# One address remainder for the first stage's matmul operands, twelve work tiles, and 8 KB for descriptors

## The chip, the core and the metric

The kernel runs as one program on one core of a Trainium2 chip. The core's engines run side by side and meet only at semaphores: TensorE (PE, with its weight loads shown apart as PEld), VectorE (DVE), ScalarE (ACT), GpSimd (POOL) and SyncE (SP). SP and POOL also issue the DMA transfers between the device memory and the on-chip memory, which has 128 partitions; a tile stands at one byte address in all of them. The metric is the device time of one execution in microseconds (us), from runs that are repeated and compared with each other.

## The reference

Two layers act on x of 2048 tokens by 1024 features, in float32, with a last RMSNorm behind them. Cut to what matters here:

```
u = rmsnorm(x, ln_g[0])
proj = u @ w_in                      # 1024 -> 3*2048 + 8: xm, z, o_pre, i_pre, f_pre
xc = silu(causal_dwconv(xm, conv_w, conv_b))
q, k = per head xc @ w_q, xc @ w_k;  v = per head xm @ w_v
h = mlstm_chunkwise(q, k, v, log_i, log_f)         # matrix memory, head by head
y = (layernorm(sigmoid(o_pre) * h) * norm_w + skip * xc) * silu(z)
x = x + y @ w_out
# second layer: rmsnorm, w_in (1024 -> 2*1536), conv, block gates, linear scan, w_out
out = rmsnorm(x, final_g)
```

The change lies in the first line of matrix work, `proj = u @ w_in`.

## The kernel before, in words

**Stages.** `phase_a1` computes the first layer's norm and `proj`, and is what this document calls the first stage; its results xm, xc = silu(conv(xm)), silu(z) and sigmoid(o) go to device memory. `phase_a2` does heads, memory and output of the first layer; the second layer and the final norm follow. The second layer uses the same class `Slab` for its big products, with `paired=True`.

**Products.** A float32 product is made of three matmuls on halves that TensorE reads as float32r: `split_into` (L806, L809) gives hi = round(t) on ACT and lo = t - hi on DVE, and `mm3` (L391 to L393) adds hi*hi, hi*lo and lo*hi into one PSUM bank. The 2x2 blocks of a matrix product go through a scheme with seven block products instead of eight. Its seven combinations of the activations, `u11 t2 t3 u21 t1 t4 u22`, are split once per half of the tokens into standing places of 2048 bytes, h and l for each of four 128-row pieces. The weights and their sums are split into a ring of eight slots (tile `s`), hi and lo one behind the other; the four sums are stored by POOL for the second half of the tokens (`keep`, L123) and fetched back by SP then (`kept`, L128).

**Wide and narrow.** `group` and `early` make xm and z: weights from a slot stand still and a 512-column place moves past them ("wide", `pa pb pc pd <- u11h..., s`). Each of the seven products is four pieces of three matmuls, 32 times: 384 matmuls, 2688 in all. `o_group` makes o and the gates: here pieces of the places stand still and 258 columns of a slot move ("narrow", `oa ob oc od <- s, u11h...`), 2688 again; its slots hold 516 columns, so `slot(516)`.

**Work tiles.** The ring `wk` of ten tiles of 516 columns holds partial sums (`p1`, `u2`, `u3`), xm with its three history columns, xc, z and the stores of o. xm, xc and z leave through POOL's queue, and a tile comes free when its store has landed.

**Order.** The tile framework's scheduler sets the order on each engine from the order in the code, from `tc.high_priority()` and from the added edges of `order`. PE, ACT, DVE, POOL and SP then each run their list in order.

**Places.** Pools are laid out upwards from address 0 behind a block of 16,384 bytes for the descriptors that POOL writes for its DMAs; the pool `tu` (the `u11` places) lies at the upper end. A tile is rounded up to a multiple of 32 bytes, so a slot of 2*516 floats takes 4128 and a tile of 516 floats 2080.

Of the kernel before, what the change touches and what calls it, by code (L numbers as in the profile page):

```python
# [7 lines left out]
F32 = mybir.dt.float32  # L8
F32R = mybir.dt.float32r
# [5 lines left out]
P = 128  # L15
# [3 lines left out]
TB = 512  # L19
# [29 lines left out]
class Slab:  # L49
# [38 lines left out]
        return (self.ta if nm in ("t3", "u22", "t1", "t4") else self.tp).tile([P, 2 * TB], dtype, tag=f"{nm}{j}", name=f"{nm}{j}")  # L88

    def wk(self, name):  # L90
        return self.rg.tile([P, 516], F32, tag="wk", name=name, bufs=10)

    def wkr(self, name):
        return self.rg.tile([P, 516], F32R, tag="wk", name=name, bufs=10)

    def psum(self, name):
        return self.pm.tile([P, 512], F32, tag="mm", name=name)

    def slot(self, w=512):

        return self.sl.tile([P, 2 * self.wide], F32R, tag="s", name="s")[:, 0:2 * w]

    def raw(self):
        return self.rw.tile([P, self.wide], F32, tag="raw", name="raw", bufs=8)[:, 0:512]
# [58 lines left out]
        return out  # L163

    def invrms(self, acc):
        rc = self.rg.tile([P, 4], F32, tag="rc", name="rc", bufs=4)
        self.K.stats_sum(self.rg, self.pm, acc if isinstance(acc, list) else [acc], rc, "mm")
        return rc

# [7 lines left out]
    def place(self, nm, j):  # L177
        if self.paired:
            self.other.pop((nm, j), None)
            t = self.pair(nm, j, F32R)  # L180
            return t[:, 0:TB], t[:, TB:2 * TB]
        n = 516 if nm == "t3" else TB
        home = self.tu if nm == "u11" else self.tp
        return tuple(home.tile([P, n], F32R, tag=f"{nm}{x}{j}", name=f"{nm}{x}{j}") for x in "hl")


    def take(self, nm, j):
# [21 lines left out]
    def temp(self, nm, x, j):  # L209

        if self.paired:
            if (nm, j) not in self.other:
                t = self.pair(nm, j)
                self.other[nm, j] = {"h": t[:, 0:TB], "l": t[:, TB:2 * TB]}
            return self.other[nm, j].pop(x)
        self.places.pop((nm, j), None)
        return self.tp.tile([P, 516 if nm == "t3" else TB], F32, tag=f"{nm}{x}{j}", name="temp")[:, 0:TB]

    def x(self):
        return self.rx.tile([P, TB], F32, tag="x", name="x", bufs=8)  # L220
# [117 lines left out]
class Trunk:  # L338
# [75 lines left out]
    def phase_a1(self, xT, woq, wxz, wout, D):  # L414
        tc, nc = self.tc, self.nc
        with ExitStack() as ctx:
            S = Slab(self, ctx, "g0")
            tp, rg, pm = S.tp, S.rg, S.pm
            wk, psum = S.wk, S.psum
            S.fix()  # L420
            G = tp.tile([P, 2, 64], F32, name="G")
            hist = tp.tile([P, 16, 3], F32, name="hist")
            nc.vector.memset(hist, 0.0)
            NE = 6
            first = [2 * m + 1 for m in range(NE)]
# [98 lines left out]
            def squares(xs, t1=False):  # L524
                acc = S.temp("t1", "l", 0) if t1 else wk("acc")[:, 0:TB]
                for k, x in enumerate(xs):
                    if k == 0:
                        nc.scalar.activation(acc, x, AF.Square)
                    else:
                        sq = S.temp("t1", "l", 1 + k % 3) if t1 else wk("sq")[:, 0:TB]  # L530
                        nc.scalar.activation(sq, x, AF.Square)
                        self.summed = nc.vector.tensor_tensor(acc, acc, sq, op=ALU.add)
                return acc
# [131 lines left out]
            for k in range(KD):  # L665
                S.scale(xs, None, pb, (k,))
                nm = ("u11", "u21")[k // 4]
# [3 lines left out]
            for s in range(2):  # L671
# [12 lines left out]
                for j, (kind, i) in enumerate(middle):  # L684
# [21 lines left out]
                    if s or j < len(middle) - 1:  # L706
                        n2 = {}
                        if s == 0 and j == len(middle) - 3:
                            rc = []
# [1242 lines left out]
```

## Time and profile before

| | |
|---|---|
| three runs | 2852.49, 2856.59, 2860.08 us (median 2856.59) |
| the profiled execution | 2854.54 us; its span from first to last instruction 2852.8 us |
| granted TensorE clock | 0.996 of full speed |
| PE busy | 2802.1 us, 98% of the span |
| DVE, ACT, POOL busy | 2131.6, 1515.6, 453.3 us (75%, 53%, 16%) |
| DMA | 687.38 MB, mean 241 GB/s |

The page gives the busy time of each engine, the span in slices, the DMA queues and the chain of waits that ended last. A matmul's duration in the profile is longer than its distance to the next one, since matmuls overlap; the distance from start to start is what a long row of them costs. A row of groups gives a mean, a row of one tile's instructions the shortest, the median and the longest.

### The profile page before, as it was taken

To read this page: it belongs to the slowest core of one execution; us is meant where nothing else is said; L and a number is where in the kernel's file an instruction comes from. 1 tells how busy PE (TensorE), PEld (TensorE's weight loads), DVE (VectorE), ACT (ScalarE), POOL (GpSimd) and SP (SyncE) were. 2 spreads that over 40 slices of the span, in tenths; PEclk is the share of its full clock that TensorE was granted. 3 is DMA by queue.
4 is the path that set the end of the run, shared out by engine and by line. 5 is a ranking of instruction groups with operands and counts; after the bars stand their busy time and mean duration, and the time that the engine had idled before them with its cause. 6 is when DMAs were issued, how large, how long until landed. Compare 5 with 4: busy or idle time off the path is not lost.

```text
span 2852.8 us, 43314 instructions
## 1 busy us (share of the span) xinstructions
PE 2802.1 (98%) x15442; PEld 2427.4 (85%) x15442; DVE 2131.6 (75%) x3657; ACT 1515.6 (53%) x2577; POOL 453.3 (16%) x846
## 2 busy tenths in 40 slices
PE   7999999999999999999999999999999999999998
PEld 5799987889997889999999988888788888788886
DVE  7767779735658688888888876678889657777774
ACT  6444545523444466666666643435444323977771
POOL 1211123111212211111121121101221111000000
PEclk9999999999999999999999999999999999999999
DMA  6756677667988765656576578776776765888866
GB/s 234 273 212 230 237 255 259 210 210 265 317 306 286 252 202 196 196 187 212 170 237 202 178 273 295 278 240 219 256 253 231 235 203 179 316 312 308 286 222 206
DMA packets 292472, 687.38 MB, mean 241 GB/s; under 512 B 29088, under 2 KB 103584, under 8 KB 292256
## 3 DMA queue, kind: packets, MB, share of 16 engines
q1 hardware_dynamic: 225072, 451.13, 49.4%
q0 software_dynamic: 66608, 232.43, 21.4%
q8 instruction: 122, 2.00, 0.3%
q10 hardware_dynamic: 576, 1.05, 0.1%
q14 instruction: 94, 0.77, 0.1%
HBM read 447.32 MB, written 237.17 MB: 240 GB/s over the span
## 4 chain that ended last, share of the span: by engine, by line
PE 80%; issue 8%; DVE 5%; ACT 2%; DMA 2%; POOL 2%; POOLq 0%; DVEq 0%; SPq 0%; ACTq 0%
PE pc L391 4%; PE pc L392 4%; PE pc L393 4%; PE pd L391 4%; PE pd L392 4%; PE pd L393 4%; PE pa L391 4%; PE pj L392 4%; PE pj L391 4%; PE pa L393 4%; PE pj L393 4%; PE pa L392 4%; PE acc L392 2%; PE acc L393 2%; PE acc L391 2%
## 5 line engine op out<-in xcount | busy, mean ns | idle before, releaser
L806 ACT CAST s<-raw 128x512 fp32r<-128x512 f32 (+1 forms) x280 | 172.7, 621 | 262.7 <-PE pd L393 74.0
L809 DVE TENSOR_TENSOR s<-raw,s 128x512 fp32r<-128x512 f32 (+1 forms) x280 | 191.7, 687 | 55.0 <-ACT s L806 54.0
L391 PE MATMUL acc<-yh,wr 128*128 128x512 f32 x384 | 148.4, 391 | 2.3 <-ACT R L1673 1.1
L392 PE MATMUL acc<-yl,wr 128*128 128x512 f32 x384 | 149.9, 390 | 0.2 <-DVE yl L809 0.2
L806 ACT CAST u<-t 128x512 fp32r<-128x512 f32 x112 | 69.1, 620 | 151.5 <-PE pc L393 47.3
L393 PE MATMUL acc<-yh,wr 128*128 128x512 f32 x384 | 149.5, 389 | 0.0
L732 DVE SCALAR_TENSOR_TENSOR xc<-xm,vec,xc 128x512 f32<-128x512 f32 x192 | 139.2, 746 | 5.6 <-ACT xc L731 4.1
L809 DVE TENSOR_TENSOR u<-t,u 128x512 fp32r<-128x512 f32 x112 | 77.1, 689 | 76.4 <-ACT u L806 76.4
L806 ACT CAST s<-sum 128x512 fp32r<-128x512 f32 (+1 forms) x120 | 74.1, 618 | 110.1 <-PE pc L393 41.3
L391 PE MATMUL pa<-u,s 128*128 128x512 f32 x304 | 119.0, 392 | 0.8 <-ACT y L1163 0.8
L393 PE MATMUL pa<-u,s 128*128 128x512 f32 x304 | 118.5, 390 | 0.1
L392 PE MATMUL pa<-u,s 128*128 128x512 f32 x304 | 118.6, 390 | 0.0
L1092 DVE SCALAR_TENSOR_TENSOR C<-C,dl,kv 128x516 f32<-128x516 f32 x112 | 83.7, 748 | 45.0 <-PE kv L393 45.0
L732 DVE SCALAR_TENSOR_TENSOR xc<-xr,vec,xc 128x512 f32<-128x512 f32 x144 | 105.8, 746 | 8.9 <-ACT xc L731 7.5
L391 PE MATMUL pj<-vwh,xmh 128*128 128x512 f32 x256 | 102.3, 402 | 0.0
L806 ACT CAST Ch<-C 128x516 fp32r<-128x516 f32 x120 | 72.5, 622 | 54.7 <-DVE da L1114 41.8
L392 PE MATMUL pj<-vwl,xmh 128*128 128x512 f32 x256 | 100.2, 391 | 0.1
L393 PE MATMUL pj<-vwh,xml 128*128 128x512 f32 x256 | 100.0, 391 | 0.0
L809 DVE TENSOR_TENSOR s<-sum,s 128x512 fp32r<-128x512 f32 (+1 forms) x120 | 82.3, 687 | 21.4 <-ACT s L806 20.5
L391 PEld LDWEIGHTS acc<-yh,wr 128*128 128x128 f32 x384 | 71.9, 188 | 19.1 <-ACT R L1673 1.6
L391 PE MATMUL pd<-u,s 128*128 128x512 f32 x224 | 87.3, 390 | 0.0
L392 PE MATMUL pd<-u,s 128*128 128x512 f32 x224 | 87.2, 389 | 0.0
(501 smaller groups left out, 10013.3 us busy)
## 6 DMA issues: line engine op xcount, KB each, us to landing
wr<-d_ow SPq DMA_DIRECT2D x96, 512.0 KB, 4.3
d_wx<-s POOLq DMA_DIRECT2D x64, 512.0 KB, 4.4
s<-d_wx SPq DMA_DIRECT2D x64, 512.0 KB, 4.7
s<-d_ws SPq DMA_DIRECT2D x64, 512.0 KB, 6.6
raw<-in_wxz_dram SPq DMA_DIRECT2D x124, 256.0 KB, 4.8
d_wr<-s POOLq DMA_DIRECT2D x48, 512.0 KB, 3.8
s<-d_wr SPq DMA_DIRECT2D x48, 512.0 KB, 4.5
raw<-in_rwin_dram SPq DMA_DIRECT2D x94, 256.0 KB, 4.2
```

The source lines that it names most:

```text
L391: mm(out, sh, mh, start=first, stop=False, skip_group_check=resumed)
L392: mm(out, sh, ml, start=False, stop=False, skip_group_check=resumed)
L393: mm(out, sl, mh, start=False, stop=last, skip_group_check=resumed)
L732: self.convd = [nc.vector.scalar_tensor_tensor(out, x[:, j:j + TB], self.v(wn, m * 4 + j), out, op0=ALU.mult, op1=ALU.add) for j in range( ...
L806: a = nc.scalar.copy(hi, src)
L809: b = (nc.gpsimd if lo_eng == "p" else nc.vector).tensor_tensor(lo, src, hi.bitcast(F32), op=ALU.subtract)
L1092: v = nc.vector.scalar_tensor_tensor(C2, C2, self.dl[:, r:r + 1], p2, op0=ALU.mult, op1=ALU.add)
```

## The change

Everything applies to the first stage alone (`paired` false), but for the last line.

1. A slot becomes 1088 floats (4352 bytes) instead of 1032 (4128). A narrow slot's contents begin 8 floats (32 bytes) into it.
2. The `t3` places are 512 floats like the others, instead of 516.
3. A work tile becomes 528 floats (2112 bytes) instead of 516 (2080 with rounding), and the ring has twelve instead of ten.
4. `hist` (the convolution's history) and `rc` (four floats of the norm, now six tiles) move into the pool `tu`, below which the `u11` places then begin 384 bytes lower.
5. The descriptor block takes 8192 bytes instead of 16,384, which pays for the larger rings.

The order of instructions on every engine is the same, row for row. What the built program's addresses come to, modulo 256:

| tile | before | after |
|---|---|---|
| t2, u21, t1, t4, u22 places | 96 | 96 |
| t3 places (eight) | 96 128 160 192 224 0 32 64 | 96 |
| u11 places | 224 | 96 |
| weight slots (eight) | 96 128 160 192 224 0 32 64 | 96 |
| narrow slots' contents | as the slots | 128 |
| raw weights, weight sums | all multiples of 32 | all multiples of 32 |
| second layer's places and slots | 96 | 96 |

```
     def wk(self, name):
-        return self.rg.tile([P, 516], F32, tag="wk", name=name, bufs=10)
+        return self.rg.tile([P, 516 if self.paired else 528], F32, tag="wk", name=name, bufs=12 - 2 * self.paired)[:, 0:516]
 
     def wkr(self, name):
-        return self.rg.tile([P, 516], F32R, tag="wk", name=name, bufs=10)
+        return self.rg.tile([P, 516 if self.paired else 528], F32R, tag="wk", name=name, bufs=12 - 2 * self.paired)[:, 0:516]
...
     def slot(self, w=512):
 
-        return self.sl.tile([P, 2 * self.wide], F32R, tag="s", name="s")[:, 0:2 * w]
+        o = 0 if w <= 512 else 8
+        return self.sl.tile([P, 1024 if self.paired else 1088], F32R, tag="s", name="s")[:, o:o + 2 * w]
...
     def invrms(self, acc):
-        rc = self.rg.tile([P, 4], F32, tag="rc", name="rc", bufs=4)
+        rc = (self.rg if self.paired else self.tu).tile([P, 4], F32, tag="rc", name="rc", bufs=4 if self.paired else 6)
...
             return t[:, 0:TB], t[:, TB:2 * TB]
-        n = 516 if nm == "t3" else TB
         home = self.tu if nm == "u11" else self.tp
-        return tuple(home.tile([P, n], F32R, tag=f"{nm}{x}{j}", name=f"{nm}{x}{j}") for x in "hl")
+        return tuple(home.tile([P, TB], F32R, tag=f"{nm}{x}{j}", name=f"{nm}{x}{j}") for x in "hl")
...
-        return self.tp.tile([P, 516 if nm == "t3" else TB], F32, tag=f"{nm}{x}{j}", name="temp")[:, 0:TB]
+        return self.tp.tile([P, TB], F32, tag=f"{nm}{x}{j}", name="temp")
...
-            hist = tp.tile([P, 16, 3], F32, name="hist")
+            hist = S.tu.tile([P, 16, 3], F32, name="hist")
...
-    nc = _bacc.Bacc("TRN2", target_bir_lowering=False, num_devices=1)
+    nc = _bacc.Bacc("TRN2", target_bir_lowering=False, num_devices=1, dynamic_dma_scratch_size=8192)
```

## The prediction

> **What bounds the kernel now.** I read the page's head first, then engine time by stage, then PE's groups in the first stage and in the second layer, then PE's waits.
>
> ```profile
> span 2852.8 us, 43314 instructions
> PE 2802.1 (98%) x15442; PEld 2427.4 (85%) x15442; DVE 2131.6 (75%) x3657; ACT 1515.6 (53%) x2577; POOL 453.3 (16%) x846
> ...
> PE 80%; issue 8%; DVE 5%; ACT 2%; DMA 2%; POOL 2%; POOLq 0%; DVEq 0%; SPq 0%; ACTq 0%
> ```
>
> ```profile
> core 0: us, PE busy (x) PEld busy (x) DVE busy (x) ACT busy (x) POOL busy (x), PEclk, DMA share, GB/s
> ...
> 20.00:993.00 973.00, 962.73 (x5435) 834.25 (x5435) 670.91 (x1319) 448.88 (x792) 192.88 (x355) 1.00 0.74 253
> 993.00:1650.00 657.00, 650.54 (x4705) 613.65 (x4705) 570.16 (x1024) 444.15 (x845) 113.77 (x244) 0.99 0.60 197
> 1650.00:2853.00 1203.00, 1184.86 (x5289) 975.86 (x5287) 881.73 (x1295) 612.40 (x926) 144.60 (x241) 1.00 0.75 255
> ```
>
> The first stage runs from about 20 to 993 us. In these 973 us PE stands still for about 10; DVE is busy for 69%, ACT for 46%, and the DMA engines for 74% of the time. PE sets this stage's length, and what one of its matmuls costs is worth its full count. A work tile or a descriptor matters only where PE waits for it.
>
> **Wide matmuls: the first stage against the second layer.** The same form, 128 rows by 512 columns with weights from a slot, at the same granted clock (1.00 in both rows above). First the groups of the first stage, then those of the second layer; the three numbers are the shortest, median and longest duration in ns:
>
> ```profile
> L391 PE MATMUL pb<-t2h,s x128: 388/394/796, 58.4 to 978.1; 128*128 128x512 f32 x128
> L392 PE MATMUL pc<-t3l,s x128: 387/394/797, 59.4 to 981.1; 128*128 128x512 f32 x128
> ...
> L393 PE MATMUL pd<-u22h,s x128: 388/394/400, 93.8 to 992.5; 128*128 128x512 f32 x128
> ```
>
> ```profile
> L391 PE MATMUL pa<-u,s x304: 387/389/504, 1658.5 to 2429.6; 128*128 128x512 f32 x152
> ...
> L393 PE MATMUL pd<-u,s x224: 389/389/390, 1747.7 to 2442.3; 128*128 128x512 f32 x112
> ```
>
> In the second layer nearly every one takes 389 ns, and 390 is the longest of 224. In the first stage the median is 394, though single ones reach 387. The program is the same there, class and all; what differs is where the tiles stand. In the second layer all places and slots begin at 96 modulo 256; in the first stage the slots run through all eight multiples of 32, and t3 and u11 stand off 96. One slot in eight happens to match. Two whole products of the first stage, the timeline's starts in us, the first with its weights in the slot at 64, the second in the slot at 96, the operand at 96 both times:
>
> ```profile
> 112.13 0.39 PE L391 MATMUL pd<-u22h,s 128*128 128x512 f32 x1
> ...
> 114.93 0.39 PE L391 MATMUL pd<-t1h,s 128*128 128x512 f32 x1
> ```
>
> ```profile
> 928.76 0.39 PE L391 MATMUL pc<-t4h,s 128*128 128x512 f32 x1
> ...
> 931.48 0.39 PE L391 MATMUL pd<-u22h,s 128*128 128x512 f32 x1
> ```
>
> Twelve matmuls in 2.80 us are 233 ns from start to start, twelve in 2.72 us are 227. Is that traffic of the other engines? A view of engine time over these two products, with a third between whose slot is at 64 too:
>
> ```profile
> 112.10:114.90 2.80, 2.80 (x13) 2.25 (x12) 1.34 (x2) 1.26 (x2) 0.98 (x2) 1.00 0.90 336
> 202.50:205.20 2.70, 2.70 (x13) 2.20 (x12) 2.63 (x10) 1.92 (x3) 0.55 (x1) 1.00 0.00 2
> 928.70:931.45 2.75, 2.75 (x14) 2.28 (x13) 2.67 (x6) 0.66 (x2) 0.71 (x2) 1.00 0.86 337
> ```
>
> The quick product has DVE busy throughout and DMA at 337 GB/s; the slow ones have DMA once at 336 and once at 2 GB/s. Neither engines nor transfers sort them; the remainder of the weights' address does. A match does not act at once: a product at 426.6 us with operand and slot both at 96 shows
>
> ```profile
> L391 PE MATMUL pc<-t4h,s 128*128 128x512 f32 x4 | 1.6, 394 | 0.0
> L392 PE MATMUL pc<-t4l,s 128*128 128x512 f32 x4 | 1.6, 393 | 0.0
> L393 PE MATMUL pc<-t4h,s 128*128 128x512 f32 x4 | 1.6, 392 | 0.0
> ```
>
> a mean of 393, between 395 and 389. Matched products seem to settle over some six to eight matmuls to an even pace and to lose it at the next mismatched slot. That is why one matching slot in eight gains little now, and why the whole ring at one remainder may gain more than eight times as much.
>
> **The change, part by part.**
>
> *Places and slots at one remainder (wide).* After the change every wide operand and every slot stands at 96 modulo 256, as in the second layer. Seven products of 384 matmuls are 2688; 394 - 389 = 5 ns each gives 13.4 us. Bounds: nothing, if placement isn't the cause; 2688 x 6 ns (233 against 227) = 16 us if most are like the product at 112 us. After waits and narrow products the pace has to settle again; the second layer has such breaks too (504 is one) and keeps its median. I take 13 us.
>
> [...]
>
> *Narrow products.* The stationary places are at 96 before and after, u11 apart; the moving contents go from mixed remainders to 128. The group rows of the first stage, the slot that happens to stand at 128 now (a stretch near 759 us), and the narrow form of the next stage:
>
> ```profile
> L391 PE MATMUL od<-s,u22h 128*128 128x258 f32 x128 | 36.2, 283 | 0.0
> L392 PE MATMUL od<-s,u22h 128*128 128x258 f32 x128 | 36.1, 282 | 0.0
> ...
> L392 PE MATMUL oa<-s,u21h 128*128 128x258 f32 x3 | 0.8, 281 | 0.0
> L393 PE MATMUL oa<-s,u21l 128*128 128x258 f32 x2 | 0.6, 282 | 0.0
> ...
> L392 PE MATMUL kv<-vl,kh 128*128 128x258 f32 x236 | 67.4, 286 | 0.4 <-DVE vl L1058 0.4
> ```
>
> The nearest row is the slot at 128: about 1 ns less on 2688 matmuls, a gain of 2.7 us. The ends: 2 ns less (281 against 283), a gain of 5.4 us; and kv, with other remainders on both sides, 3.5 ns more, a loss of 9.4 us. I take a gain of 3, by the nearest row.
>
> *Twelve work tiles.* Waits in the first stage for a tile whose store is on its way:
>
> ```profile
> PE oa L391 <- ACT p L591: 1.9, 3, 0.7
> ...
> ACT p L591 <- DMA d_xm<-xm: 11.3, 3, 5.1
> ```
>
> ACT has to copy the first narrow partial sum into a work tile whose xm is still being stored; it is late by up to 5.1 us, and behind it PE waits for PSUM three times. With two more tiles the store has about two tiles' time longer. Of 1.9 us and the weight loads and the pace lost around it I take 2; the bounds are 0 and 3. What the copy then waits for is PE's own product, as at its other calls.
>
> *Descriptor block.* Half the room for what POOL writes per DMA:
>
> ```profile
> L641 POOL DMA_DIRECT2D d_sz<-z x64 | 35.0, 547 | 181.4 <-ACT z L639 181.4
> ...
> q0 software_dynamic: 66608, 232.43, 21.4%
> d_xm<-xm POOLq DMA_DIRECT2D x64, 256.0 KB, 4.9
> ```
>
> POOL spends 0.55 us on an issue and lands it 4.9 us later; in the first stage it is busy for 193 of 973 us and waits for ACT's results, not for room. I cost it at nothing. That cover is POOL's idle time: were each issue to wait for the landing before it, the stage's 355 POOL rows (x355 above), nearly all DMAs, would need 355 x 5.4 = 1900 us, twice the stage; with two in flight 960, about the stage; with four 480, hidden again.
>
> *The rest.* `hist` and `rc` are the same instructions on another address: nothing. No instruction moves on any engine. In the next stages all pools keep their remainder; the tiles that take over first-stage addresses at 993 us are freed by other tiles than before. PE loses about 6 us in that whole stage, and I see no term there.
>
> **Sum.** 13 + 3 + 2 = 18 us off the profiled execution's own 2854.5 us is 2836.5. The median of the three runs, 2856.6, stands 2 us above that execution; against it I forecast 2838 us.
>
> **The rivals.**
>
> *A. As above*: 2838, own range 2832 to 2844. For it: the exact pace in one matching product and in the whole second layer. Chance 0.82.
>
> *B. Placement does nothing for PE here.* The even pace would come from something else that the second layer has. Then the work tiles' 2 us are all: 2854 to 2855. Against it: the three windows above. Chance 0.06. [...]
>
> *C. The narrow products lose what the wide ones gain in part.* At 128 they go to the pace of kv: 13 + 2 - 9.4 = about 6 us, 2851. For it: kv's own remainders cost it 3 to 4 ns. Against: the slot at 128. Chance 0.05.
>
> *D. Another engine takes up half of it.* PE comes 1.8% sooner to each product, and splits by ACT and DVE or transfers become the last to arrive: about 9 us, 2847. Against: 10 us of PE waits in 973, DVE at 69%; DMA at 74% would go to 75%. Chance 0.04.
>
> *E. Slower: the descriptor room holds back POOL's queue.* With fewer than two DMAs in flight, work tiles come free later, ACT's p copies and with them PE wait at each of the eight `o_group` calls for a landing, 4.9 us: 39 us on 2838, about 2877. It decides from the point at which issue to landing over the number in flight exceeds 973 / 355 = 2.7 us. For it: the room is halved. Against: POOL's idle time is put down to ACT throughout. Chance 0.03.
>
> **How the numbers follow.** A measurement of this kernel tells about 0.3%, 8.6 us, from no change. Faster by more than that: A, most of D: 0.85. Within it: B, C and the rest of D: 0.12. Slower: E, 0.03. The range 2829 to 2849 takes in the narrow products at their best (16 + 5.4 + 3 = 24.4 us off, and 3 to 4 us by which the three runs stray from their median) below and D above; outside it lie B, C and E with 0.14, and little of A.
>
> **What would show it.** Wide groups of the first stage at a median of 389 with a shortest of 388 or 389, and the stage's end near 975 us instead of 993: right. Medians of 391 to 393: the pace settles only in part. Narrow groups at 281 or 282 means: right; 285 and above is C. No row of PE or ACT p waiting on d_xm: the twelve tiles. POOL issues still at 0.54 us, with no row in which POOL waits on its own DMAs: the descriptor block at nothing. A stage that shortens by 18 us with later stages that lengthen would make the forecast wrong in a place that I cost at nothing.

## The result, and the profile after

The changed kernel takes 2841.22 us (median of six runs, 2838.34 to 2844.68); the kernel before, run beside it, 2855.07 us (six runs, 2851.08 to 2860.08). The ratio is 0.9952, with a 95% interval of 0.9943 to 0.9962: faster by 13.9 us, where 18 were forecast and 2838 us predicted. The profiled execution is the shortest of the six, 2838.34 us; the profiled one before took 2854.54. Between these two, from which the accounts below are made, lie 16.2 us.

The head of the page of the changed kernel: span, busy time of each engine, and the chain of waits.

```profile
span 2836.6 us, 43324 instructions
PE 2785.1 (98%) x15442; PEld 2421.6 (85%) x15442; DVE 2129.8 (75%) x3657; ACT 1515.7 (53%) x2577; POOL 451.8 (16%) x846
...
PE 81%; DVE 7%; issue 5%; DMA 3%; ACT 2%; POOL 1%; POOLq 0%; DVEq 0%; SPq 0%; ACTq 0%
```

PE is busy for 17 us less with the same 15442 matmuls; DVE, ACT and POOL do what they did. The view of engine time by stage, with the first stage cut at 975 us, where the prediction wanted its end:

```profile
core 0: us, PE busy (x) PEld busy (x) DVE busy (x) ACT busy (x) POOL busy (x), PEclk, DMA share, GB/s
20.00:975.00 955.00, 944.55 (x5420) 828.41 (x5419) 665.59 (x1313) 446.82 (x789) 191.82 (x353) 1.00 0.75 256
975.00:1632.00 657.00, 649.82 (x4716) 612.68 (x4715) 572.57 (x1028) 444.97 (x846) 112.42 (x244) 1.00 0.61 198
1632.00:2836.00 1204.00, 1186.10 (x5294) 976.42 (x5292) 882.24 (x1296) 613.06 (x926) 145.52 (x243) 1.00 0.74 255
```

The granted clock is 1.00 in this stage as before. 5420 matmuls fit into these 955 us, where the kernel before had 5435 in 973. The first matmul of the second stage starts at 978.4 us; before, at 992.8. So 14.4 of the 16.2 us come from the first stage. The wide groups, shortest, median and longest duration in ns:

```profile
L391 PE MATMUL pb<-t2h,s x128: 389/389/796, 58.3 to 964.1; 128*128 128x512 f32 x128
L392 PE MATMUL pc<-t3l,s x128: 389/389/793, 59.3 to 967.0; 128*128 128x512 f32 x128
...
L393 PE MATMUL pd<-u22h,s x128: 388/389/397, 94.2 to 978.2; 128*128 128x512 f32 x128
```

These are the second layer's 389, in place of 394. The narrow ones in the view that gives busy time and mean duration:

```profile
L391 PE MATMUL od<-s,u22h 128*128 128x258 f32 x128 | 36.0, 282 | 0.0
...
L392 PE MATMUL od<-s,u22h 128*128 128x258 f32 x128 | 36.0, 281 | 0.0
...
L393 PE MATMUL od<-s,u22l 128*128 128x258 f32 x128 | 35.8, 280 | 0.0
```

**Start to start.** Durations overlap: a wide matmul of the changed kernel lasts 389 ns in the median, and the next one starts 227 ns after it. What PE pays is the distance from one matmul's start to the next. I worked it out for the 2688 wide and the 2688 narrow matmuls of each trace. A distance of 300 ns or more after a wide one, of 150 or more after a narrow one, is called a pause (what it has over the pace counts); the mean of the others is the pace.

| | before | after | difference in the stage |
|---|---|---|---|
| wide pace | 232.34 ns | 227.33 ns | -13.5 us |
| narrow pace | 119.94 ns | 118.89 ns | -2.8 us |
| pauses between narrow matmuls | 3.6 us (7) | 1.1 us (4) | -2.5 us |
| pauses between wide matmuls | 16.1 us (49) | 21.3 us (69) | +5.2 us |
| first product starts at | 19.9 us | 19.3 us | -0.7 us |

Before rounding the sum is -14.4, as is the shift of the stage's end. The first three rows are the prediction's three terms, 13, 3 and 2. The fourth it did not have. The waits of PE's weight loads in the first stage (total us, times, longest) say who is late, first before, then after:

```profile
PEld oa L391 <- ACT p L591: 2.5, 3, 0.9
...
PEld pa L391 <- ACT p L312: 0.7, 3, 0.3
...
PEld pd L391 <- DVE xm L302: 0.5, 2, 0.3
```

```profile
PEld pa L391 <- ACT p L312: 1.6, 5, 0.5
...
PEld pd L391 <- DVE xm L302: 1.2, 3, 0.6
```

The wait for the work tile (`p` of L591) is gone. The waits for a copy or an add that empties a PSUM bank have grown, each short: the two rows shown by 1.6 us together. The rest of the 5.2 us is spread over many short pauses. One of the grown waits in the timeline of the changed kernel (start and length in us, engine):

```profile
205.02 1.53 DVE L732 SCALAR_TENSOR_TENSOR xc<-xm,vec,xc 128x512 f32<-128x512 f32 x2
...
206.46 0.68 DVE L302 TENSOR_TENSOR xm<-pd,p 128x512 f32<-128x512 f32 x1
...
207.20 0.19 PEld L391 LDWEIGHTS pd<-u22h,s 128*128 128x128 f32 x1 [0.56 <-DVE xm L302]
```

PE wants to write bank `pd` again, but DVE first does two steps of the convolution (1.53 us) and only then the add that empties the bank (0.68 us); PE's weight load waits 0.56 us for it. In the kernel before, the same add ended at 207.16 us and the weight load started at 207.84, without a wait: here the PE that comes sooner waits longer. That the other pauses grew for the same reason is not shown one by one.

In the rest of the program the two executions differ by 2.6 us in the second stage and by 0.8 us, the other way, behind it. That is not the change: among the kernels below, which leave the second stage alone, its length differs by more than that.

### The profile page after: what moved, and what is told of

Its sections match the earlier page's. It is cut to its first block, busy times and chain, and to the rows that moved or that the text cites. A ratio compares the mean times of both kernels' runs of the same rounds, so it can differ in the third digit from the quotient of the medians.

```text
span 2836.6 us, 43324 instructions
## 1 busy us (share of the span) xinstructions
PE 2785.1 (98%) x15442; PEld 2421.6 (85%) x15442; DVE 2129.8 (75%) x3657; ACT 1515.7 (53%) x2577; POOL 451.8 (16%) x846
## 4 chain that ended last, share of the span: by engine, by line
PE 81%; DVE 7%; issue 5%; DMA 3%; ACT 2%; POOL 1%; POOLq 0%; DVEq 0%; SPq 0%; ACTq 0%
PE pc L391 4%; PE pd L391 4%; PE pc L392 4%; PE pc L393 4%; PE pd L393 4%; PE pd L392 4%; PE pj L392 4%; PE pj L391 4%; PE pj L393 4%; PE pa L391 4%; PE pa L393 4%; PE pa L392 4%; PE acc L392 2%; PE acc L393 2%; PE acc L391 2%
## 5 line engine op out<-in xcount | busy, mean ns | idle before, releaser
L391 PE MATMUL pa<-u,s 128*128 128x512 f32 x304 | 119.0, 392 | 0.8 <-ACT y L1163 0.8
L809 DVE TENSOR_TENSOR s<-sum,s 128x512 fp32r<-128x512 f32 (+1 forms) x120 | 82.3, 687 | 20.3 <-ACT s L806 19.9
L391 PEld LDWEIGHTS acc<-yh,wr 128*128 128x128 f32 x384 | 71.9, 188 | 19.8 <-DMA wr<-d_ow 1.9
```

What stands on the lines that cost most here:

```text
L391: mm(out, sh, mh, start=first, stop=False, skip_group_check=resumed)
L809: b = (nc.gpsimd if lo_eng == "p" else nc.vector).tensor_tensor(lo, src, hi.bitcast(F32), op=ALU.subtract)
```

## The experiments

Each kernel ran in three or five rounds beside the kernel before, whose median was between 2855.9 and 2856.4 us. Each edit is against the changed kernel unless it says otherwise. The differences named for narrow blocks are bytes by which a block's address stands beyond that of the stationary place, modulo 256.

| kernel | wide: slot against place | narrow blocks | tiles | wide pace, ns | narrow pace, ns | pauses, wide / narrow, us | stage ends, us | median, us | ratio to before (95%) |
|---|---|---|---|---|---|---|---|---|---|
| before | mixed | mixed | 10 | 232.34 | 119.94 | 16.1 / 3.6 | 992.8 | 2855.07 | |
| after | same | 32 to 56 | 12 | 227.33 | 118.89 | 21.3 / 1.1 | 978.4 | 2841.22 | 0.9952 (0.9943 to 0.9962) |
| slots at 64 | 224 | 32 to 56 | 12 | 233.28 | 119.03 | 17.5 / 1.1 | 991.2 | 2853.83 | 0.9995 (0.9986 to 1.0004) |
| slots alternate | same, 128 | mixed | 12 | 230.42 | 120.15 | 19.8 / 1.0 | 988.3 | 2850.36 | 0.9982 (0.9973 to 0.9991) |
| all at 0 | same | 32 to 56 | 12 | 227.22 | 118.90 | 21.7 / 1.1 | 978.6 | 2837.56 | 0.9941 (0.9926 to 0.9956) |
| all at 0, again | same | 32 to 56 | 12 | 227.25 | 118.90 | 22.4 / 1.1 | 979.4 | 2839.42 | 0.994 (0.9926 to 0.9953) |
| ten tiles | same | 32 to 56 | 10 | 227.22 | 118.90 | 21.4 / 4.5 | 981.6 | 2843.51 | 0.9958 (0.9944 to 0.9972) |
| before, twelve tiles | mixed | mixed | 12 | 232.32 | 120.02 | 17.5 / 1.0 | 991.4 | 2853.03 | 0.999 (0.9981 to 0.9999) |
| before, 8 KB | mixed | mixed | 10 | 232.28 | 119.94 | 17.8 / 2.8 | 992.7 | 2856.45 | 0.9997 (0.9988 to 1.0006) |
| narrow at 0 | same | 0 to 24 | 12 | 227.24 | 122.70 | 21.3 / 1.0 | 988.7 | 2852.00 | 0.9989 (0.998 to 0.9997) |
| narrow at 64 | same | 64 to 88 | 12 | 227.22 | 120.04 | 23.0 / 1.0 | 984.1 | 2846.11 | 0.9962 (0.9949 to 0.9976) |
| narrow at 224 | same | 224 to 248 | 12 | 227.40 | 119.05 | 21.2 / 1.1 | 979.1 | 2841.53 | 0.9948 (0.9936 to 0.9961) |
| narrow, two pieces | same | 32, 40 | 12 | 227.16 | 120.00 | 26.8 / 1.0 | 986.7 | 2848.59 | 0.9972 (0.9963 to 0.9982) |
| narrow, four pieces | same | 32 | 10 | 227.25 | 120.00 | 27.9 / 21.8 | 1009.1 | 2871.39 | 1.0055 (1.0041 to 1.0069) |

### What the wide products need: slots at 64, slots that alternate, everything at 0

*Slots at 64.* All wide contents begin 224 bytes into the slot, so that every slot stands at 64 and every place at 96. Everything else is the change.

```
-        o = 0 if w <= 512 else 8
+        o = (0 if self.paired else 56) if w <= 512 else 8
```

> The changed kernel, but the wide contents begin 224 bytes into their slot, so all wide weights stand at 64 modulo 256 against operand places at 96; nothing else moves. Theory P (what counts is that weights and moving operand share one remainder modulo 256): the wide medians go from 389 back to 394 or 395, the stage by 2640 x 5 to 6.6 ns = 13 to 17 us, 2854 to 2858 us in all. Rival C (it is enough that all slots share one remainder with each other, whichever): medians stay at 389 and the time at 2841. Rival N (the gain came from the ring sizes or the descriptor block): 2841 as well.

*Slots that alternate.* Slots of 4224 bytes, which stand at 96 and 224 in turn; the places stay at 96.

```
-        return self.sl.tile([P, 1024 if self.paired else 1088], F32R, tag="s", name="s")[:, o:o + 2 * w]
+        return self.sl.tile([P, 1024 if self.paired else 1056], F32R, tag="s", name="s")[:, o:o + 2 * w]
```

> The changed kernel, but a slot takes 4224 bytes, so the eight slots stand at 96 and 224 modulo 256 in turn, all at 96 modulo 128; places at 96. Theory P with a period of 256: about half of the wide products match and settle only late in their twelve matmuls, the others run at 232 to 233 ns from start to start; a mean near 231, some 10 to 12 us lost, 2851 to 2854 us. Rival with a period of 128: medians 389, 2841 us.

*Everything at 0.* Two pads move all places and slots of the first stage, and of the second layer, to remainder 0.

```
+        self.pad = cp.tile([P, 40], F32, name="pad")
+        nc.vector.memset(self.pad, 0.0)
...
+            nc.vector.memset(S.tu.tile([P, 24], F32, name="padu"), 0.0)
```

> The changed kernel, but 160 bytes of padding ahead of the low pools and 96 in the upper pool, so places and slots of the first stage, and those of the second layer, stand at 0 modulo 256, equal to each other. Theory P (only the equality counts): medians 389 in both, 2841 us within 3. Rival A (the remainder 96 itself counts): medians near 394 in the first stage and in the second layer, (2688 + 5088) x 5 ns = 39 us more, 2880 us.

One wide group of each, in this order (shortest, median, longest duration in ns; first and last start):

```profile
L391 PE MATMUL pd<-u22h,s x128: 393/396/505, 94.3 to 990.5; 128*128 128x512 f32 x128
```

```profile
L391 PE MATMUL pd<-u22h,s x128: 387/392/504, 93.9 to 987.6; 128*128 128x512 f32 x128
```

```profile
L393 PE MATMUL pd<-u22h,s x128: 387/389/499, 94.0 to 978.0; 128*128 128x512 f32 x128
```

Slots that all stand at one remainder, but not at that of the places, give no quick pace: 396 ns in the median, slower even than the mixed ring's 394. So it isn't that the addresses stay the same from slot to slot. With alternating slots half the matmuls have a match: those 1356 are 228.2 ns apart, the other 1269, at a distance of 128 bytes, 232.8. So the period is not 128; and half a ring of matches gives about half of what lies between the slots at 64 (233.3) and the change (227.3). Nor is the period longer than 256: the changed kernel's slots are 17 x 256 bytes apart, so that neighbours differ by 256 modulo 512, and the pace over all of them is 227.3 ns. Everything at 0 keeps the pace of 227.2, and the second layer, which was moved with it, its 389, so it is not remainder 96 itself. What is left is the prediction's cause: weights and moving operand with one remainder modulo 256 gave the quick pace, 227.2 to 227.3 ns here. The slots at 64 have the change's twelve tiles, narrow placing and descriptor room as well, and with them no more than a ratio of 0.9995: the tiles and the narrow products earn little more than the wide pace loses against the mixed ring. All three medians lie just under what the theory of equal remainders expected, by 0.2 to 0.6 us.

An equal remainder is not the only good one, though. The ring of the kernel before runs through all eight differences; by the addresses of the built program its wide matmuls have these paces:

| slot minus place, modulo 256 | 0 | 32 | 64 | 96 | 128 | 160 | 192 | 224 |
|---|---|---|---|---|---|---|---|---|
| pace in the kernel before, ns | 229.7 | 232.7 | 233.0 | 233.5 | 232.7 | 233.2 | 230.1 | 233.5 |

The two other kernels with a mixed ring agree: with twelve tiles 229.5 at 0 and 230.8 at 192, with 8 KB alone 229.6 and 230.0. So a slot 64 bytes below its operand is nearly as quick there as one at the same remainder. No run has a whole ring at 192; what pace it would settle to is open.

### The work tiles and the descriptor room

*Ten tiles.* The change with ten work tiles of 528 floats; a pad keeps the remainders.

```
-        return self.rg.tile([P, 516 if self.paired else 528], F32, tag="wk", name=name, bufs=12 - 2 * self.paired)[:, 0:516]
+        return self.rg.tile([P, 516 if self.paired else 528], F32, tag="wk", name=name, bufs=10)[:, 0:516]
...
+            nc.vector.memset(rg.tile([P, 32], F32, tag="pad", name="padr", bufs=1), 0.0)
```

> The changed kernel with ten work tiles instead of twelve and a pad that keeps every remainder. If the two tiles are worth what the first trace's waits say, PE's waits for the copy of the first narrow partial sum come back, 2 to 3 us: 2843 to 2845 us, with the wide medians at 389. If they are worth nothing: 2841. If the gain was theirs and not the places': 2853.

The waits come back, of PE and, behind it, of ACT (from 600 us to the stage's end):

```profile
PE oa L391 <- ACT p L592: 2.1, 4, 0.7
```

```profile
ACT p L592 <- DMA d_xm<-xm: 9.3, 2, 4.7
```

Narrow pauses are 4.5 us against 1.1, the stage ends 3.2 us later, the median is 2.3 us higher.

*The kernel before with twelve tiles* (of 516 floats, remainders mixed as before) *and 8 KB.*

```
-        return self.rg.tile([P, 516], F32, tag="wk", name=name, bufs=10)
+        return self.rg.tile([P, 516], F32, tag="wk", name=name, bufs=10 if self.paired else 12)
...
+    nc = _bacc.Bacc("TRN2", target_bir_lowering=False, num_devices=1, dynamic_dma_scratch_size=8192)
```

> The kernel before with twelve work tiles in place of ten and the descriptor room of 8 KB that makes place for them; places, slots and remainders stay mixed as before. Theory P (the tiles are worth the waits they remove, 2.5 us between the two profiled executions, 2.3 us between the changed kernel and the run with ten): 2852.5 to 2854, ratio 0.999, and no pause of 0.2 us or more between two narrow products. Rival T (the tiles only pay once PE runs faster): no change, 2855 to 2856.

*The kernel before with 8 KB alone* has only the last line of that edit.

> The kernel before with the descriptor room halved to 8 KB and nothing else; every address goes down by 8192 bytes, 32 times 256, so all remainders stay. Theory P (the gain is the addresses and the two work tiles): no change, 2855 to 2856, ratio 0.999 to 1.001, POOL's time from issue to landing as before. Rival E (the smaller room holds POOL): slower, 2860 or more. Rival S (the room carries part of the gain): 2853 or less.

Twelve tiles alone are worth 3.2 us (2853.03 against 2856.25; interval 0.3 to 5.4), as expected; narrow pauses fall from 3.6 to 1.0 us. The smaller descriptor room changes nothing that can be measured (0.9988 to 1.0006). The trace shows the smaller room all the same. The timeline of one of POOL's issues and of the DVE instruction that it waits for, first before, then with 8 KB:

```profile
175.24 0.68 DVE L809 TENSOR_TENSOR s<-sum,s 128x512 fp32r<-128x512 f32 x1
...
176.22 0.53 POOL L123 DMA_DIRECT2D d_wx<-s  x1 [5.21 <-DVE s L809]
```

```profile
175.74 0.69 DVE L809 TENSOR_TENSOR s<-sum,s 128x512 fp32r<-128x512 f32 x1
...
177.98 0.55 POOL L123 DMA_DIRECT2D d_wx<-s  x1 [6.47 <-issue]
```

Before, POOL issues 0.3 us after DVE ended; with 8 KB 1.55 us after, and what held it the profile does not show. A `d_sz` near 578 us is late in the same way by about 1.3 us, and the changed kernel has both as well (6.42 us idle at 176.78, 3.48 at 572.05). The kernel before, the only one with 16 KB, shows neither. So the smaller room seems to hold POOL twice in the stage, by 1.3 us each time, though the two kernels with narrow pieces (below), which have 8 KB too, do not show it at these places. The time shows no cost of it.

The parts add up: addresses with ten tiles 12.4 us (2855.92 - 2843.51) and tiles 3.2, each with the smaller room in it, are 15.6, beside the 13.9 of the whole; that is within what the intervals leave open.

### The narrow products

In the changed kernel the pace of a narrow matmul goes by its block: 115.9 ns at a difference of 32 bytes, 120.8 at 40, 121.6 at 48, 118.4 at 56. If that were a property of the difference, other placings would give more. Three runs asked this.

*Narrow at 0*: the contents at the start of the slot, at the places' own remainder.

```
-        o = 0 if w <= 512 else 8
+        o = 0
```

> The changed kernel with the narrow contents at the start of the slot, 32 bytes lower, so that their four blocks lie 0, 8, 16 and 24 bytes beyond the places' remainder instead of 32, 40, 48 and 56. Theory O (a narrow product's spacing goes by the difference of the remainders, 115.9, 120.8, 121.6 and 118.4 ns for the latter four): by the means of these differences in the kernel before (119.1, 120.1, 120.4, 117.9 ns) a narrow mean of 119.4 ns, 1.4 us more than the changed kernel, 2842 to 2844. Rival Q (the four values belong to the product's position in the order, not to the address): the same four values, 118.9 ns, 2841. Rival M (equal remainders are fastest here as in the wide products): the blocks at difference 0 at 115.9 ns or less, 2841 or less.

*Two pieces*: both blocks of the high parts at 32, both of the low parts at 40 (the lines that use the slot follow suit).

```
+        t = self.sl.tile([P, 1024 if self.paired else 1152], F32R, tag="s", name="s")
...
+        return t.rearrange("p (n r) -> p n r", n=2)[:, :, 8:524]
```

> The changed kernel with the narrow contents as two pieces of 516 elements 576 apart in slots of 1152: both blocks of the high parts (two products of three) 32 bytes beyond the places' remainder, both of the low parts 40 beyond. Order of work unchanged on every engine. Theory O: 1792 narrow products at 115.9 and 896 at 120.8 ns, mean 117.5, 3.7 us less than the changed kernel: 2837 to 2838. Rival Q: mean 118.9, 2841.

*Four pieces*: all four blocks at 32.

```
+        t = self.sl.tile([P, 1024 if self.paired else 1280], F32R, tag="s", name="s")
...
+        return t.rearrange("p (n r) -> p n r", n=4)[:, :, 8:266]
```

> All four narrow blocks 32 bytes beyond the places' remainder (pieces of 258 elements 320 apart, slots of 1280); for the room that this takes the ring has ten work tiles, as in the run with ten, 2843.5. Theory O: narrow mean 115.9 ns, 8 us less than that run, less or nothing of it lost to DVE and ACT, which write the blocks and take the same time: 2835 to 2837. Rival Q: 118.9 ns, 2843 to 2844.

None of the three came out as any theory had it. With all blocks at 32 each narrow matmul takes 120.0 ns, not 115.9; with two pieces 119.2, 123.5 and 117.4 ns in turn, which is 120.0 again. So a block's own difference does not set the distance in these runs: 32 bytes came with 115.9 ns among four differences and with 120.0 alone. The distance went with how the differences follow each other. The narrow contents at 0 are slower by 3.8 ns a matmul, 10.2 us in the stage and 10.8 us in the median. The view of engine time over 30 us inside groups of narrow products, first the changed kernel, then the one at 0 (rows that overlap the edges are counted, some two too many):

```profile
152.00:182.00 30.00, 30.00 (x255) 30.00 (x254) 14.64 (x33) 11.94 (x25) 4.27 (x8) 1.00 0.67 240
212.00:242.00 30.00, 30.00 (x255) 30.00 (x254) 20.63 (x44) 13.99 (x28) 5.91 (x11) 1.00 0.81 292
```

```profile
152.00:182.00 30.00, 30.00 (x244) 30.00 (x243) 13.43 (x30) 11.82 (x24) 4.23 (x8) 1.00 0.64 232
222.00:252.00 30.00, 30.00 (x255) 30.00 (x254) 17.58 (x38) 12.28 (x24) 4.27 (x8) 1.00 0.66 234
750.00:780.00 30.00, 30.00 (x243) 30.00 (x242) 16.84 (x36) 10.88 (x22) 5.95 (x12) 1.00 0.90 309
```

At 0 there are two paces, 124.4 and 118.9 ns by the starts. All eight groups of 336 matmuls begin at the slow one. Five keep it to their end (first and third row). In the other three, PE's list cuts the second product after 19 matmuls, in the middle of a triple, and puts the 48 of another product in between:

```profile
219.86 0.28 PE L393 MATMUL ob<-s,t2l 128*128 128x258 f32 x1
219.97 0.28 PE L391 MATMUL ob<-s,t2h 128*128 128x258 f32 x1
220.09 0.28 PE L391 MATMUL oa<-s,u21h 128*128 128x258 f32 x1
```

Up to this cut the three groups run at 123.9 ns, from it to their end at 118.9 to 119.0 (second row). So the pace goes with the order of the matmuls and not by chance: all three groups with the cut turn quick at it, and the five without it stay slow. The changed kernel has the same three cuts and one pace, 118.9 to 119.0, in all eight groups. Why the cut changes the pace is open. At 1.00 in all rows, the clock has no part in it, nor have the other engines or the traffic: the quick row lies between the two slow ones in DMA (0.66 against 0.64 and 0.90), and above both in DVE (17.58 us against 13.43 and 16.84).

The two kernels with pieces also lose elsewhere. Two pieces lengthen the wide pauses to 26.8 us. With four, POOL's stores of the weights, whose rows are now four pieces of 1032 bytes, land in 10.3 us, where the kernel with ten tiles needs 5.8 in the same stretch (235 to 350 us; issues, KB each, median us to landing), first ten tiles, then four pieces, with PE's largest wait there:

```profile
d_wq<-s POOLq DMA_DIRECT2D x16, 516.0 KB, 5.8
```

```profile
d_wq<-s POOLq DMA_DIRECT2D x15, 516.0 KB, 10.3
```

```profile
PE od L402 <- DVE os L591: 8.1, 2, 4.1
```

That the slow stores hold up DVE, and DVE PE, is what these rows suggest; it was not tried apart. The time of this kernel says nothing on the narrow pace; its trace does.

*Narrow at 64 and at 224* ask where the bad placing ends: `o = 16` and `o = 56` in the same line.

> The changed kernel with the narrow contents 64 bytes into the slot, so that their four blocks lie 64, 72, 80 and 88 bytes beyond the places' remainder. Theory N1 (a narrow block must only not begin at the places' own remainder, which costs 3.8 ns a product in the run with 0 to 24): a narrow mean of 119 ns, 2841. Rival N2 (it goes by the value of the difference, and 32 to 56 is one of the good ones): by the means of these differences in the kernel before (119.5, 122.0, 118.7, 119.8 ns) 120.3 ns, 3.7 us more, 2844 to 2846; as much more again if it grows in the steady state as it did at 0 to 24, 2848.

> The same with 224 bytes: differences 224, 232, 240 and 248. Theory N1: a narrow mean of 119 ns, 2841. Rival N2: by the means of these differences in the kernel before (118.1, 120.9, 119.9, 119.3 ns) 119.5 ns, 1.7 us more, 2842 to 2844, or away from this as at 0 to 24 (up to 122.7 ns, 2851).

At 64 the pace is 120.0 ns and the median 2846.11 us; at 224 it is 119.0 ns and 2841.53 us. Both theories are half right: 224 does as well as 32, 64 costs 3.1 us of pace, where the means of the mixed kernel said 3.7. No placing of the four found a pace under 118.9.

### A kernel that beats both?

Everything at remainder 0 had the lowest ratio of all, so it ran once more, unchanged.

> The kernel with all places and slots at remainder 0 once more, since its ratio in three rounds (0.9941, interval 0.9926 to 0.9956) and that of the changed kernel (0.9952, 0.9943 to 0.9962) overlap. Theory P (only the difference of the remainders counts, and it is the same in both): 0.9945 to 0.9955 of the kernel before, 2840 to 2842. Rival Z (remainder 0 itself is worth something more): 0.9941 again, 2838 to 2839.

It came to 0.994 again. Its intervals (0.9926 to 0.9956, 0.9926 to 0.9953) overlap with the changed kernel's (0.9943 to 0.9962), and the traces show no place for a gain: wide 227.2 ns, narrow 118.9, the stage's end at 978.6 and 979.4 us against 978.4 us. It may be better by some 3 us; this is not shown, and where they would come from stays open.

## Why the prediction was right, step by step

- **What bounds the stage.** Right. With PE's pace alone moved by slots at 64, the stage ends at 991.2 us instead of 978.4.
- **Wide, 13 us.** Right: 13.5 us measured, by the cause that was named. One step in it was incomplete: "one slot in eight happens to match" overlooks that the slots at a difference of 192 were nearly as quick as the matched ones (230.1 and 229.7 ns), so in the mixed ring about a quarter of the wide matmuls, not an eighth, were quicker than the rest. The runs show that the weights' place counts beside the operand's: 233.3 ns with the weights 224 bytes from the operand, 227.2 with both at 0 and 227.3 with both at 96, for one form (128x512) at a granted clock of 1.00 in all three. With that rival B, by which placement does nothing for PE here, has fallen.
- **That the pace settles** over six to eight matmuls. The changed kernel's trace bears it out: behind the pause at 206.67 us one distance of 337 ns and six of 229 to 236 follow, and 227 from 208.93 us on. The cost of settling is small: with half the slots matched, the matched ones still came to 228.2 ns in the mean.
- **Narrow, 3 us.** 2.8 us measured, but that is luck: the step that gave it was not a sound one. It took the five matmuls of two rows, of the one slot that stood at 128, for what the whole would do. The run at 0 shows a loss of 7.4 us against the kernel before (2688 x 2.76 ns), in the upper part of the bounds and near rival C's 9.4. The 32 bytes by which the change shifts the narrow contents decide between a gain of 3 us and a loss that takes back half of the wide products' gain. The trace of before hardly told the two apart (119.0 and 119.4 ns by its means for these differences); the bounds held the measured time, the working did not.
- **Twelve tiles, 2 us.** 2.5 us between the profiles, 2.3 and 3.2 us by medians of two pairs of kernels. Right, by the wait that was named.
- **Descriptor room at nothing.** Right: 0.4 us the other way, interval across zero. POOL's issues are late twice in the stage, by 1.3 us; whether by rival E's mechanism isn't shown. Its price of 39 us has fallen: the run with 8 KB alone shows no cost.
- **The rest at nothing.** Here the forecast lost its 4 us. The rival that another engine takes up half of the gain (D) was set as a case of its own, 9 us at a chance of 0.04; it is a term that belongs in the sum. Pauses between wide products grew by 5.2 us against the one trace of before, by 3.5 to 3.8 against the three other kernels at the slow pace. They grow with the pace, whatever else is changed: 17.5 to 17.8 us in the three kernels with 232 to 233 ns run beside, 19.8 with 230.4, 21.2 to 23.0 in all those with 227 and whole narrow slots. DVE and ACT are no busier (2129.8 and 1515.7 us, 2131.6 and 1515.6 before). In the case shown it is the order on DVE, where a convolution stands ahead of an add that PE waits for, and PE now comes sooner; the others were not followed one by one. With 4 to 5 us for this term the forecast of 18 becomes 13 to 14, beside 13.9 measured. The "10 us of PE waits in 973" that spoke against D were those of the slower PE.
- **What would show it.** The medians (389), the narrow means (280 to 282), the missing waits and POOL's issues (534 to 547 ns in the mean) came as listed; the stage's end at 978 instead of 975 is the missed term.

## What to carry to other kernels

Where matmuls of one form run at two paces at one granted clock, compare the addresses of the weights and of the moving operand modulo 256: for products of 512 columns a common remainder was worth 5 to 6 ns of 233, and half the tiles matched gave half of it (230.4 ns, between 233.3 and 227.3). It is the best placing that was run as a whole, not the only good one. For shorter rows there is no such rule in these runs, so try two or three offsets and keep the best. When the bounding engine gets quicker by some 2%, add to the sum what it will wait for next: here the short waits that it already had grew by 3.5 to 5 us of the 18.8 that the three terms gained.

## What the runs showed of the hardware that was not expected

- Wide matmuls, 128x512 at a granted clock of 0.99 to 1.00, kept 227.2 to 227.4 ns where weights and operand share the remainder modulo 256. They took 232.8 ns at a distance of 128 bytes and 233.3 at 224; the remainder's own value made no difference (227.2 ns with both at 0, 227.2 to 227.4 with both at 96). In the mixed ring of the kernel before, a distance of 192 was nearly as quick as 0 (230.1 and 229.7 ns), and the six others took 232.7 to 233.5.
- Narrow matmuls of 258 columns kept a pace that went by how their blocks follow each other, for up to 336 matmuls: 118.9 ns on average with blocks at differences of 32 to 56 bytes, 119.0 at 224 to 248, 120.0 at 64 to 88, 120.0 evenly with all at 32, and at 0 to 24 either 124.4 ns or, once the row has been cut after 19 matmuls of a product, 118.9 to 119.0. Why equal remainders gave the quickest pace that was run for 512 columns (227.2 ns) and, without the cut, a row that begins at one the slowest of the four placings here (124.4 ns) is open.
- Halving the room for descriptors from 16 to 8 KB cost nothing measurable (ratio 0.9997, 0.9988 to 1.0006) with POOL's 355 rows in 973 us; in every trace with 8 KB and whole slots two issues come after 6.4 to 6.7 and 3.5 to 3.6 us of idle time that the profile puts down to `issue`, with 8 KB alone some 1.3 us late each. A store whose rows are four pieces of 1032 bytes instead of one of 4128 landed in 10.3 us instead of 5.8.
